# Eight experts on one core: b1 as eight rows with one-pass transposes, and a last piece of w2 of 128 columns

## The chip, the core and the metric

The kernel runs on one core of one Trainium2 chip. The metric is the device time of one execution in microseconds. A core has a matrix engine (TensorE, in the profile PE, with its weight loads as PEld), a vector engine (VectorE, DVE), an activation engine (ScalarE, ACT), GpSimd (POOL), a sync engine (SP), and 16 DMA engines that move data between the device memory and the on-chip memory. TensorE writes only to an accumulator memory (PSUM), from which VectorE or ScalarE copy. Transfers are issued by SP, ScalarE and GpSimd; in the profile an issue stands under SPq, ACTq or POOL.

## The reference

Eight experts, each with 256 rows of tokens, a hidden size of 512 and an inner size of 2,048:

```python
n_experts, capacity, hidden, expert_hidden = 8, 256, 512, 2048

def reference(x, w1, w2, b1, b2):
    h = np.matmul(x, w1) + b1[:, np.newaxis, :]
    h = np.maximum(h, 0)
    return (np.matmul(h, w2) + b2[:, np.newaxis, :]).astype(np.float32)
```

All inputs are float32. w1 and w2 are 4 MB each per expert, 64 MB in all eight.

## The kernel before

The weights are cast to float16 by the transfer that loads them, which GpSimd issues. For each expert x is transposed on TensorE, the first product is made transposed, so that its bias b1 is one number per partition and can go into ScalarE's Relu, and the second product starts from b2. The second product lags three experts behind the first.

b1 has to stand with its 2,048 values of an expert over 128 partitions and 16 columns (`b1T`). It is loaded as 16 rows of 1,024 (each expert's row in two halves) and turned by 32 products with an identity, each of which gives 64 partitions:

```python
b1_rows = singles.tile([E * 2, M // 2], fp32)
b1T = singles.tile([P, nJ, E], fp32)
...
x32 = singles.tile([P, nXF32, nTB, H], fp32)
for e in range(nXF32):      # the first two experts' x, as float32
    (nc.sync if e == 0 else nc.scalar).dma_start(out=x32[:, e], max_dma_last_dim=2048, in_=...)
nc.scalar.dma_start(out=b1_rows, in_=b1.rearrange("e (s i) -> (e s) i", s=2))
load_w1(0)
...
pb = psum_x.tile([P, nJ, E, 2], fp32, tag="psx", name="pb")
for j in range(nJ):                                          # nJ = 16
    for s in range(2):
        ordered(nc.tensor.matmul(                            # L194
            out=pb[s * 64 : (s + 1) * 64, j, :, :],
            lhsT=b1_rows.rearrange("r (q j) -> r q j", j=nJ)[:, :, j],
            rhs=ident[0 : 2 * E, 0 : 2 * E],
            start=True, stop=True,
        ))
for s in range(2):
    nc.vector.tensor_copy(                                   # L202
        out=b1T[s * 64 : (s + 1) * 64, :, :], in_=pb[s * 64 : (s + 1) * 64, :, :, s]
    )
transposes(0)                                                # L97, then the copy to xT in L103
```

The w2 of the last expert comes in six pieces (rows `lo` to `hi` of its 16 per partition, columns `c0` to `c1`), the last two of which share the same rows and split the columns. HH is 256, half of the 512 columns:

```python
for lo, hi, c0, c1 in (
    (0, 4, 0, H), (4, 8, 0, H), (8, 12, 0, H), (12, 14, 0, H),
    (14, 16, 0, HH), (14, 16, HH, H),
):
    t = w2t_pool.tile([P, hi - lo, c1 - c0], fp16, ...)
    ordered(nc.gpsimd.dma_start(out=t, in_=src[:, lo:hi, c0:c1]))       # L90
    w2_sb[e].append((lo, hi, c0, c1, t))
```

The second product of the last expert keeps the same two column blocks in separate accumulators, so every row of the earlier pieces gives two matmuls, one for each block. A block is stored as soon as its last piece is through:

```python
blocks = [(0, HH, psum_o, "po"), (HH, H, psum_h, "ph")]      # e == E - 1
...
for lo, hi, p0, p1, t in w2_sb[e]:
    mine = [b for b in blocks if p0 <= b[0] and b[1] <= p1]
    for tb in range(nTB):                                    # nTB = 2
        for j in range(lo, hi):
            for c0, c1, _, _ in mine:
                ordered(nc.tensor.matmul(                    # L163
                    out=acc[c0, tb],
                    lhsT=hT[e][:, j, tb * P : (tb + 1) * P],
                    rhs=t[:, j - lo, c0 - p0 : c1 - p0], ...))
    if hi == nJ:
        for c0, c1, _, _ in mine:
            store(e, [acc[c0, tb] for tb in range(nTB)], c0, c1, e == E - 1)

def store(e, po, c0, c1, split):
    ...
    nc.vector.tensor_copy(out=out_sb[:, 0, :], in_=po[0])    # L130
    nc.scalar.copy(out=out_sb[:, 1, :], in_=po[1])           # L131
    if split:                                                # the last expert
        nc.sync.dma_start(out=dst[:, 0, :], in_=out_sb[:, 0, :])      # L134
        nc.scalar.dma_start(out=dst[:, 1, :], in_=out_sb[:, 1, :])    # L135
    else:
        nc.sync.dma_start(out=dst, in_=out_sb)               # L137
```

Of the kernel before, what the change touches and what calls it, by code (L numbers as in the profile page):

```python
# [11 lines left out]
def kernel(  # L12
# [9 lines left out]
    nc = tc.nc  # L22
    fp32 = mybir.dt.float32
    fp16 = mybir.dt.float16
    E, T, H = x.shape
    M = w1.shape[2]
    P = 128
    nTB = T // P
    nKC = H // P
    nJ = M // P  # L30
    HH = H // 2
    LAG = 3
    nXF32 = 2

    def ordered(ins):
        return tc.keep_in_program_order(ins)

    singles = ctx.enter_context(tc.tile_pool(name="singles", bufs=1))
# [7 lines left out]
    psum_x = ctx.enter_context(tc.tile_pool(name="psum_x", bufs=1, space=bass.MemoryType.PSUM))  # L46
    psum_h = ctx.enter_context(tc.tile_pool(name="psum_h", bufs=3, space=bass.MemoryType.PSUM))
    psum_o = ctx.enter_context(tc.tile_pool(name="psum_o", bufs=2, space=bass.MemoryType.PSUM))

    ident = singles.tile([P, P], fp32)  # L50
    ident16 = singles.tile([P, P], fp16)
    ones1 = singles.tile([1, P], fp16)
    b2_sb = singles.tile([1, E * H], fp16)
    b1_rows = singles.tile([E * 2, M // 2], fp32)
    b1T = singles.tile([P, nJ, E], fp32)

    x16 = [None] * E
# [11 lines left out]
    def load_w1(e):  # L69
        w1_sb[e] = w1_pool.tile([P, nKC, M], fp16, tag="w1", name="w1sb")  # L70
        ordered(nc.gpsimd.dma_start(  # L71
            out=w1_sb[e], in_=w1[e].rearrange("(p kc) m -> p kc m", kc=nKC)
        ))

    def load_w2(e):
        src = w2[e].rearrange("(p j) h -> p j h", j=nJ)
        w2_sb[e] = []
        if e < E - 1:
            t = w2_pool.tile([P, nJ, H], fp16, tag="w2", name="w2sb")
            step = nJ if e < E - 2 else nJ // 2  # L80
            for lo in range(0, nJ, step):
                ordered(nc.gpsimd.dma_start(out=t[:, lo : lo + step, :], in_=src[:, lo : lo + step, :]))  # L82
                w2_sb[e].append((lo, lo + step, 0, H, t[:, lo : lo + step, :]))
            return
        for lo, hi, c0, c1 in (
            (0, 4, 0, H), (4, 8, 0, H), (8, 12, 0, H), (12, 14, 0, H),
            (14, 16, 0, HH), (14, 16, HH, H),
        ):
            t = w2t_pool.tile([P, hi - lo, c1 - c0], fp16, tag=f"w2_{lo}_{c0}", name=f"w2_{lo}_{c0}")
            ordered(nc.gpsimd.dma_start(out=t, in_=src[:, lo:hi, c0:c1]))  # L90
            w2_sb[e].append((lo, hi, c0, c1, t))

    def transposes(e):
        pt = psum_x.tile([P, nKC, T], fp16, tag="psx", name="psx")
        for kc in range(nKC):
            for tb in range(nTB):
                ordered(nc.tensor.transpose(  # L97
                    out=pt[:, kc, tb * P : (tb + 1) * P],
                    in_=x16[e][:, tb, :].rearrange("p (q kc) -> p q kc", kc=nKC)[:, :, kc],
                    identity=ident16,  # L100
                ))
        xT[e] = xT_pool.tile([P, nKC, T], fp16, tag="xT", name="xT")
        nc.vector.tensor_copy(out=xT[e], in_=pt)  # L103
# [23 lines left out]
    def store(e, po, c0, c1, split):  # L127
        w = c1 - c0
        out_sb = out_pool.tile([P, nTB, w], fp32, tag=f"out{w}", name=f"out{w}")
        nc.vector.tensor_copy(out=out_sb[:, 0, :], in_=po[0])  # L130
        nc.scalar.copy(out=out_sb[:, 1, :], in_=po[1])  # L131
        dst = out[e].rearrange("(p tb) h -> p tb h", tb=nTB)[:, :, c0:c1]
        if split:
# [5 lines that stand above are left out]
    def second_product(e):  # L139
        if e < E - 1:  # L140
            blocks = [(0, H, psum_o, "po")]
        else:
            blocks = [(0, HH, psum_o, "po"), (HH, H, psum_h, "ph")]
        acc = {}
        for c0, c1, pool, tag in blocks:
            for tb in range(nTB):
                t = pool.tile(
                    [P, c1 - c0], fp32, tag=tag if tag == "ph" else f"{tag}{tb}", name=f"acc{tb}"
                )
                acc[c0, tb] = t  # L150
                ordered(nc.tensor.matmul(  # L151
                    out=t,
                    lhsT=ones1,
                    rhs=b2_sb[0:1, e * H + c0 : e * H + c1],
                    start=True,
                    stop=False,
                ))
        for lo, hi, p0, p1, t in w2_sb[e]:
            mine = [b for b in blocks if p0 <= b[0] and b[1] <= p1]
            for tb in range(nTB):  # L160
# [5 lines that stand above are left out]
                            rhs=t[:, j - lo, c0 - p0 : c1 - p0],  # L166
                            start=False,
                            stop=(j == nJ - 1),
# [5 lines that stand above are left out]
    x32 = singles.tile([P, nXF32, nTB, H], fp32)  # L174
    for e in range(nXF32):
        (nc.sync if e == 0 else nc.scalar).dma_start(out=x32[:, e], max_dma_last_dim=2048, in_=x[e].rearrange("(p tb) h -> p tb h", tb=nTB))
    nc.scalar.dma_start(out=b1_rows, in_=b1.rearrange("e (s i) -> (e s) i", s=2))
    load_w1(0)
    ordered(nc.gpsimd.dma_start(  # L179
        out=b2_sb,  # L180
        in_=b2.rearrange("e h -> (e h)").rearrange("(o f) -> o f", o=1),
# [6 lines left out]
        x16[e] = x_pool.tile([P, nTB, H], fp16, tag="x16", name="x16")  # L188
        nc.vector.tensor_copy(out=x16[e], in_=x32[:, e])  # L189

    pb = psum_x.tile([P, nJ, E, 2], fp32, tag="psx", name="pb")
    for j in range(nJ):
        for s in range(2):
            ordered(nc.tensor.matmul(  # L194
                out=pb[s * 64 : (s + 1) * 64, j, :, :],
                lhsT=b1_rows.rearrange("r (q j) -> r q j", j=nJ)[:, :, j],
                rhs=ident[0 : 2 * E, 0 : 2 * E],
                start=True,
                stop=True,
            ))  # L200
    for s in range(2):
        nc.vector.tensor_copy(  # L202
            out=b1T[s * 64 : (s + 1) * 64, :, :], in_=pb[s * 64 : (s + 1) * 64, :, :, s]
        )
    transposes(0)

    loads = []
    for s in range(1, E + LAG):
        if s < E:
            if s >= nXF32:  # L210
                loads.append((load_x, s))
            loads.append((load_w1, s))
        if s >= LAG:
            loads.append((load_w2, s - LAG))
# [8 lines left out]
    for s in range(E + LAG):  # L223
        issue_until(lambda: (
            (min(s + 2, E - 1) < E and w1_sb[min(s + 2, E - 1)] is not None)
            and (s + 2 < LAG or w2_sb[min(s + 2 - LAG, E - 1)] is not None)
        ))
        if s < E:
            first_product(s)
        if s >= LAG:  # L230
            second_product(s - LAG)
# [30 lines left out]
```

## Time and profile before

| | |
|---|---|
| time, median of 3 | 186.09 us (185.63 to 186.1) |
| span of the profiled execution | 183.9 us |
| TensorE busy | 138.5 us (75%) |
| ScalarE busy | 62.8 us (34%) |
| VectorE busy | 13.4 us (7%) |
| read from device memory | 71.39 MB |
| written to device memory | 4.19 MB |

The profile is of one execution, and its span begins and ends somewhat inside the timed interval. Its page has a picture of the span in 40 slices, in which each digit is the busy share of a slice in tenths, and the row DMA is the mean over the 16 DMA engines. GB/s and packet sizes count the bytes as written, so a weight that is read as float32 and written as float16 counts half. The queues: q0 is what GpSimd issues, q1 what SP issues, q10 what ScalarE issues. The timeline gives instructions in order of time: start, duration, engine, line, operation, what it writes and reads, shape, count, and in brackets the idle time of the engine before it with what ended it. The ends of matmuls are modelled: they are pipelined, so that a new one starts long before the one before it has ended in the record.

### The profile page before, as it was taken

How to read it: one execution, taken by the hardware profiler on the slowest of the kernel's cores; microseconds unless marked ns; L12 is line 12 of the kernel's file. 1: busy time of each engine (PE TensorE's matmuls, PEld its weight loads, DVE VectorE, ACT ScalarE, POOL GpSimd, SP SyncE). 2: the span in 40 equal slices, each digit the busy share in tenths (PEclk: the TensorE clock that was granted, in tenths of full speed). 3: DMA queues.
4: the chain of work that ended last, by engine and by line, in shares of the span. 5: the costliest groups of instructions: out<-in, count | busy, mean ns of one | idle time of the engine just before them, and what ended most of it. 6: DMA issues, size and time to landing. Idle time of an engine off the chain costs nothing.

```text
span 183.9 us, 2209 instructions
## 1 busy us (share of the span) xinstructions
PE 138.5 (75%) x946; PEld 99.0 (54%) x946; DVE 13.4 (7%) x22; ACT 62.8 (34%) x138; POOL 16.9 (9%) x37
## 2 busy tenths in 40 slices
PE   0546969397571999529995499917999997999971
PEld 0634969396451846427465464815648842434760
DVE  0320101001000100001010101001010010101001
ACT  0022869477360513605126150622506901010101
POOL 7100030301100012000110000100006200000000
PEclk9999999999875699965999789995799999999998
DMA  5998999899998999899999999999899998999993
GB/s 185 286 221 180 228 228 224 174 229 230 228 217 182 228 228 228 178 278 217 196 214 236 270 203 203 228 271 228 185 228 228 211 275 198 237 243 257 217 211 114
DMA packets 6488, 40.57 MB, mean 221 GB/s; under 512 B 688, under 2 KB 1728, under 8 KB 4432
## 3 DMA queue, kind: packets, MB, share of 16 engines
q0 software_dynamic: 4320, 35.14, 91.3%
q1 hardware_dynamic: 1568, 4.46, 6.6%
q10 hardware_dynamic: 592, 0.85, 1.3%
q8 instruction: 7, 0.11, 0.2%
q14 instruction: 1, 0.01, 0.0%
HBM read 71.39 MB, written 4.19 MB: 411 GB/s over the span
## 4 chain that ended last, share of the span: by engine, by line
DMA 57%; PE 31%; another core or an unknown queue 5%; POOL 3%; issue 1%; ACT 0%; ACTq 0%; POOLq 0%
DMA x<-in_x_dram 25%; DMA w<-in_w_dram 19%; PE ph L110 16%; DMA w1sb<-in_w_dram 12%; PE acc L163 12%; PE psx L97 2%; PE acc L151 1%; POOL w2sb L82 1%; POOL w L90 1%; POOL w1sb L71 1%; ACT out L131 0%; POOL b_sb L179 0%; POOL ident masks.py:199 0%; ACTq L135 0%
## 5 line engine op out<-in xcount | busy, mean ns | idle before, releaser
L110 PE MATMUL ph<-xT,w1sb 128*128 128x256 f16 x512 | 69.3, 302 | 11.8 <-DMA w1sb<-in_w_dram 11.8
L117 ACT ACTIVATE hT<-ph,b1T 128x256 f16<-128x256 f32 x128 | 57.1, 475 | 47.4 <-PE ph L110 47.1
L110 PEld LDWEIGHTS <-w1sb 128*128 128x128 f16 x512 | 62.0, 149 | 18.5 <-DMA w1sb<-in_w_dram 12.8
L163 PE MATMUL acc<-w2sb,hT 128*128 128x512 f16 x224 | 49.7, 379 | 1.5 <-DMA w2sb<-in_w_dram 1.5
L163 PEld LDWEIGHTS <-hT 128*128 128x128 f16 x288 | 27.5, 98 | 32.0 <-issue 6.5
L131 ACT COPY out<-acc 128x512 f32<-128x512 f32 (+1 forms) x9 | 4.9, 541 | 59.7 <-PE acc L163 59.7
L97 PE MATMUL psx<-ident,x 128*128 128x128 f16 x64 | 6.8, 269 | 20.6 <-DMA x<-in_x_dram 20.0
L97 PEld LDWEIGHTS <-x 128*128 128x128 f16 x64 | 5.3, 128 | 21.7 <-DMA x<-in_x_dram 20.9
L103 DVE COPY xT<-psx 128x1024 f16<-128x1024 f16 x8 | 5.5, 692 | 84.3 <-PE psx L97 84.3
L130 DVE COPY out<-acc 128x512 f32<-128x512 f32 (+1 forms) x9 | 5.7, 632 | 74.0 <-PE acc L163 73.9
L71 POOL DMA_DIRECT2D w1sb<-in_w_dram x8 | 4.4, 554 | 67.9 <-PE ph L110 67.1
L82 POOL DMA_DIRECT2D w2sb<-in_w_dram x8 | 4.3, 536 | 57.1 <-PE acc L163 57.1
L194 PE MATMUL pb<-ident,b_rows 16*64 16x16 f32 x64 | 3.7, 266 | 6.4 <-DMA b_rows<-in_b_dram 6.4
L163 PE MATMUL acc<-w,hT 128*128 128x256 f16 x64 | 7.6, 272 | 1.2 <-DMA w<-in_w_dram 1.2
L194 PEld LDWEIGHTS pb<-ident,b_rows 16*64 16x64 f32 x64 | 3.6, 198 | 6.4 <-issue 6.4
L117 ACT ACT_TABLE_LOAD x1 | 1.3, 1283 | 10.9 <-DVE b1T L202 10.9
L151 PE MATMUL acc<-b_sb,ones 1*128 1x512 f16 (+1 forms) x18 | 4.8, 355 | 0.0
L90 POOL DMA_DIRECT2D w<-in_w_dram x6 | 3.6, 614 | 12.4 <-DMA w2sb<-in_w_dram 12.4
L65 POOL DMA_DIRECT2D x<-in_x_dram x6 | 3.3, 546 | 2.2 <-DMA w1sb<-in_w_dram 2.2
L151 PEld LDWEIGHTS <-ones 1*128 1x128 f16 x18 | 1.1, 92 | 2.1 <-issue 2.1
L189 DVE CAST x<-x 128x1024 f16<-128x1024 f32 x2 | 1.4, 698 | 4.3 <-DMA x<-in_x_dram 4.3
L202 DVE COPY b1T<-pb 64x128 f32<-64x128 f32 x2 | 0.6, 288 | 3.5 <-PE pb L194 3.5
(8 smaller groups left out, 2.0 us busy)
## 6 DMA issues: line engine op xcount, KB each, us to landing
w1sb<-in_w_dram POOLq DMA_DIRECT2D x8, 2048.0 KB, 33.6
w2sb<-in_w_dram POOLq DMA_DIRECT2D x6, 2048.0 KB, 47.0
out_dram<-out SPq DMA_DIRECT2D x7, 512.0 KB, 8.0
w2sb<-in_w_dram POOLq DMA_DIRECT2D x2, 1024.0 KB, 24.3
x<-in_x_dram POOLq DMA_DIRECT2D x6, 256.0 KB, 39.9
w<-in_w_dram POOLq DMA_DIRECT2D x3, 512.0 KB, 31.8
x<-in_x_dram ACTq DMA_DIRECT2D x1, 512.0 KB, 5.2
x<-in_x_dram SPq DMA_DIRECT2D x1, 512.0 KB, 4.5
```

Of the source, the lines that this page charges most:

```text
L71: ordered(nc.gpsimd.dma_start(out=w1_sb[e], in_=w1[e].rearrange("(p kc) m -> p kc m", kc=nKC)))
L82: ordered(nc.gpsimd.dma_start(out=t[:, lo : lo + step, :], in_=src[:, lo : lo + step, :]))
L90: ordered(nc.gpsimd.dma_start(out=t, in_=src[:, lo:hi, c0:c1]))
L97: ordered(nc.tensor.transpose(out=pt[:, kc, tb * P : (tb + 1) * P], in_=x16[e][:, tb, :].rearrange("p (q kc) -> p q kc", kc=nKC)[:, :, kc] ...
L103: nc.vector.tensor_copy(out=xT[e], in_=pt)
L110: ordered(nc.tensor.matmul(out=ph, lhsT=w1_sb[e][:, kc, :].rearrange("p (q j) -> p q j", j=nJ)[:, :, j], rhs=xT[e][:, kc, :], start=(kc == 0),
L117: nc.scalar.activation(out=hT[e][:, j, :], in_=ph, func=mybir.ActivationFunctionType.Relu, bias=b1T[:, j, e : e + 1], scale=1.0,)
L130: nc.vector.tensor_copy(out=out_sb[:, 0, :], in_=po[0])
L131: nc.scalar.copy(out=out_sb[:, 1, :], in_=po[1])
L151: ordered(nc.tensor.matmul(out=t, lhsT=ones1, rhs=b2_sb[0:1, e * H + c0 : e * H + c1], start=True, stop=False,))
L163: ordered(nc.tensor.matmul(out=acc[c0, tb], lhsT=hT[e][:, j, tb * P : (tb + 1) * P], rhs=t[:, j - lo, c0 - p0 : c1 - p0], start=False, sto ...
L194: ordered(nc.tensor.matmul(out=pb[s * 64 : (s + 1) * 64, j, :, :], lhsT=b1_rows.rearrange("r (q j) -> r q j", j=nJ)[:, :, j], rhs=ident[0 ...
```

## The change

Two things change. b1 is loaded as eight rows of 2,048, one per expert, and turned by 16 transposes, each of which fills all 128 partitions, so one VectorE copy takes the result. This is meant to shorten the work on TensorE ahead of the first product. And the two last pieces of the last w2 are of 384 and 128 columns in place of 256 and 256, and so are the two column blocks and the stores. This is meant to leave less work behind the piece that lands last.

```diff
-    HH = H // 2
+    HN = H - P
...
-    b1_rows = singles.tile([E * 2, M // 2], fp32)
+    b1_rows = singles.tile([E, M], fp32)
...
-            (14, 16, 0, HH), (14, 16, HH, H),
+            (14, 16, 0, HN), (14, 16, HN, H),
...
-            blocks = [(0, HH, psum_o, "po"), (HH, H, psum_h, "ph")]
+            blocks = [(0, HN, psum_o, "po"), (HN, H, psum_h, "ph")]
...
-    nc.scalar.dma_start(out=b1_rows, in_=b1.rearrange("e (s i) -> (e s) i", s=2))
+    nc.scalar.dma_start(out=b1_rows, in_=b1)
...
-    pb = psum_x.tile([P, nJ, E, 2], fp32, tag="psx", name="pb")
+    pb = psum_x.tile([P, nJ, E], fp32, tag="psx", name="pb")
     for j in range(nJ):
-        for s in range(2):
-            ordered(nc.tensor.matmul(
-                out=pb[s * 64 : (s + 1) * 64, j, :, :],
-                lhsT=b1_rows.rearrange("r (q j) -> r q j", j=nJ)[:, :, j],
-                rhs=ident[0 : 2 * E, 0 : 2 * E],
-                start=True,
-                stop=True,
-            ))
-    for s in range(2):
-        nc.vector.tensor_copy(
-            out=b1T[s * 64 : (s + 1) * 64, :, :], in_=pb[s * 64 : (s + 1) * 64, :, :, s]
-        )
+        ordered(nc.tensor.transpose(
+            out=pb[:, j, :],
+            in_=b1_rows.rearrange("r (q j) -> r q j", j=nJ)[:, :, j],
+            identity=ident[0:E, 0:E],
+        ))
+    nc.vector.tensor_copy(out=b1T, in_=pb)
     transposes(0)
```

## The prediction

> **What bounds the kernel now.** I read the page's second part first, for which resource is full over the whole span.
>
> ```profile
> PE   0546969397571999529995499917999997999971
> DMA  5998999899998999899999999999899998999993
> DMA packets 6488, 40.57 MB, mean 221 GB/s; under 512 B 688, under 2 KB 1728, under 8 KB 4432
> q0 software_dynamic: 4320, 35.14, 91.3%
> q1 hardware_dynamic: 1568, 4.46, 6.6%
> q10 hardware_dynamic: 592, 0.85, 1.3%
> ```
>
> The row DMA is at 8 or 9 tenths in every slice but the first and the last, while TensorE (PE) has slices with 3, 1 and 2 tenths. The three queue lines sum to 99.2% of the time of 16 engines. So the transfers are the bound from about 4 us to about 178 us. The packet records of the trace say the same when packets in flight are counted per microsecond: between 16.0 and 19.9 in every microsecond from 3 to 178. Work off the DMA engines can then only matter at the two ends: before the first weights land, and after the last.
>
> The timeline of the first 16 us shows the first end.
>
> ```profile
> 5.26 1.41 DVE L189 CAST x<-x 128x1024 f16<-128x1024 f32 x2 [4.27 <-DMA x<-in_x_dram]
> 6.44 3.72 PE L194 MATMUL pb<-ident,b_rows 16*64 16x16 f32 x64 [6.44 <-DMA b_rows<-in_b_dram]
> 10.20 0.59 DVE L202 COPY b1T<-pb 64x128 f32<-64x128 f32 x2 [3.53 <-PE pb L194]
> 10.84 1.04 PE L97 MATMUL psx<-ident,x 128*128 128x128 f16 x8 [0.69 <-DVE b1T L202]
> 11.92 0.69 DVE L103 COPY xT<-psx 128x1024 f16<-128x1024 f16 x1 [1.13 <-PE psx L97]
> 15.52 0.61 PEld L110 LDWEIGHTS <-w1sb 128*128 128x128 f16 x4 [3.90 <-DMA w1sb<-in_w_dram]
> ```
>
> Columns: start, duration, engine, line, what, and in brackets the idle time before with its releaser. The turn of b1 (L194), its copy, and the transposes of x are over at 11.92 + 0.69 = 12.61 us. The first product then waits until 15.52 for w1 of the first expert. There are 15.52 - 12.61 = 2.91 us of slack behind this chain.
>
> The timeline of the last 9 us shows the other end.
>
> ```profile
> 175.77 1.91 PE L163 MATMUL acc<-w,hT 128*128 128x256 f16 x16 [0.73 <-DMA w<-in_w_dram]
> 178.12 1.95 PE L163 MATMUL acc<-w,hT 128*128 128x256 f16 x16 [0.44 <-DMA w<-in_w_dram]
> 179.41 0.90 DVE L130 COPY out<-acc 128x256 f32<-128x256 f32 x2 [9.52 <-PE acc L163]
> 179.63 0.37 ACT L131 COPY out<-acc 128x256 f32<-128x256 f32 x1 [8.13 <-PE acc L163]
> 179.86 0.81 SPq L134 DMA_DIRECT2D out_dram<-out  x2
> 180.03 0.37 ACTq L135 DMA_DIRECT2D out_dram<-out  x1
> 180.44 0.37 ACT L131 COPY out<-acc 128x256 f32<-128x256 f32 x1 [0.44 <-PE acc L163]
> 180.84 0.35 ACTq L135 DMA_DIRECT2D out_dram<-out  x1
> ```
>
> From 178.12 TensorE runs 16 matmuls: 8 on the piece of rows 12 to 14, which it had waited for, 4 on the first half-width piece and 4 on the last. The starts are 0.109 us apart. The only larger step is before the 13th, the first on the last piece: 179.317 to 179.470, which is 0.044 us too much. The last packet of the weight stream ends at 179.156, and 0.31 us from there is 179.47. So the last landing and TensorE's own backlog meet within 0.05 us. After that ScalarE works strictly in order: copy, issue, copy, issue. Its second copy could have begun when the last matmul ended, at 179.795 + 0.272 = 180.07, but begins at 180.44, because the first copy and its issue hold the engine until 180.40. The last issue ends at 180.84 + 0.35 = 181.19, the last store's packets run from 181.83 to 182.38, and the span ends at 183.93, 1.55 us later.
>
> **What the Trainium skill says.** "DMA: Bandwidth & Descriptors", section "Why a DMA increments its semaphore by 16 and not by 1", says a copy is spread over the largest number of engines up to 16 that divides the slowest dimension of both sides. The trace agrees as far as it goes: b1 as 16 rows is 16 packets of 4,096 bytes of 159 ns each. By the rule 8 rows go to 8 engines, 8 KB each; no run shows that yet. The same page's "Specifications" give 512 bytes as the least size for full rate. The trace has weight packets of 512 bytes as written (60 ns) and larger, none smaller; the change brings some of 256. "TensorE: Matmul & The Clock Gate", section "Back-to-back issue gap", puts a warm matmul of N columns at N/2.4 + 2.5 ns: 109 ns for 256, just what the tail shows. I use it for 384 columns (162 ns); for 128 it gives 56 ns, and the trace's eight transposes of 128 columns in the chain at 30.37 us take 0.45/8 = 56 ns.
>
> **The change, part by part.**
>
> *b1 on TensorE.* The 64 records of L194 take 3.72 us, 58 ns each: 32 products in two passes. After: 16 one-pass transposes. At 58 ns that is 0.93 us; doubled, for weight loads of 128 columns in place of 64, 1.9 us. One VectorE copy of 128 partitions, about 0.29 us, replaces two (0.59 us together). So xT is ready 2.1 to 3.1 us sooner, at about 9.5 to 10.5 us. All of it lies in front of the wait for w1, which ends at 15.52 either way. Gain on the path: 0.
>
> *b1 on the DMA engines.* If 8 engines carry 8 KB in place of 4, each has one more 159 ns of work ahead of the weight stream, and the other eight have 159 ns less. Every weight load is spread over all 16 and waits for the slowest, and they never run empty until 178 us, so a lag at the start is still there at the end. Whether it counts depends on which engines finish last. In the microsecond after 178 there are 10.2 in flight on average, and 0.9 in the one after 179, so engines differ by up to 1.3 us at the end, and packets do not carry an engine's name. Between 0 and +0.16 us; I take +0.08.
>
> *The stream of w2.* The last 512 packets per 1 KB read become 256 of 1.5 KB and 256 of 512 bytes. The packets written as 512, 2,048, 4,096, 8,192 and 16,384 bytes took 60, 172, 324, 624 and 1,227 ns: 22 ns plus 0.0735 ns per byte. So 768 bytes should cost 79 ns and 256 bytes 41 ns. Per engine: 16 x 79 + 16 x 41 = 1.92 us, against 32 x 60 = 1.92 us. The last landing stays at 179.47, and the piece before it lands 0.3 us later than now, still ahead of the 4 matmuls that need it at 179.0.
>
> *TensorE at the end.* 8 matmuls of the 12 to 14 piece: 4 x (162 + 56) = 872 ns, against 8 x 109. Then 4 x 162 = 650 ns, in place of 436, which puts the first store's blocks later by 0.21 us. The last piece would start at 178.12 + 0.872 + 0.650 = 179.64, now past the landing at 179.47, so the wait of 0.044 us goes. Last start 179.64 + 3 x 0.056 = 179.81, ending 0.053 us sooner after it than a 256-column one: about 180.03, against 180.07.
>
> *ScalarE.* Its copies take 372 ns for 256 columns and 590 ns for 512 (page groups kept apart by shape): 0.85 ns per column, so about 480 for 384 and 264 for 128; the sum is the same. It starts its first copy at 179.63 + 0.21 = 179.84 and does copy, issue, copy, issue in the same total: last issue ends at 181.19 + 0.21 = 181.40. This is the term that counts: **the path runs through ScalarE's first copy, which waits for more columns than before, not through the last landing.**
>
> *The stores.* The last store shrinks from 128 packets of 1 KB (0.54 us from first start to last end) to 128 of 512 bytes. If it has the engines to itself, it takes about 0.35 us and gives back 0.19 of the 0.21. But all four stores run from 180.69 to 182.38 with the engines busy almost throughout: 32 packets of 47 ns per engine are 1.5 of those 1.69 us, and the total of bytes is unchanged. If the engines are the limit, the end moves with the first store, which starts later by 0.11 (VectorE's copy waits for the first tb block) + 0.13 (557 in place of 424 ns) = 0.24 us. So +0.02 to +0.25; I take +0.12.
>
> Sum: 0 + 0.08 + 0 + 0.12 = +0.20 us. **186.09 + 0.2 = 186.3 us.**
>
> **Rivals.**
> 1. *The short tail pays.* If the last landing is what sets the end, everything behind it shrinks: 4 x 53 ns of matmul, 0.05 of latency, 0.11 of copy, 0.19 of store, about 0.55 us, giving 185.5. For it: the 13th matmul does wait 0.044 us for the landing. Against: ScalarE's second copy waits for ScalarE, 0.37 us past its input.
> 2. *Small packets cost more.* If a packet of 256 bytes written costs as much as one of 512 (60 ns), the stream ends 16 x 19 = 0.3 us later; TensorE has 0.17 us in hand there, and ScalarE 0.7, so most is still hidden. At twice 60 ns, 16 x 79 = 1.26 us later, about 0.4 of which would show past ScalarE's chain: 186.7. No packet below 512 bytes in the weight stream speaks for or against.
> 3. *The start counts.* If the first product began with b1 and not with w1, 2 to 3 us would be gained: 183.5. The idle of 3.90 us in front of L110, released by a DMA, is against it.
> 4. *Fewer instructions.* The queue of instruction fetches moves seven packets of 16 KB, about 0.9 us each, on engines that also carry weights. Some 100 records fewer may shift or save one: plus or minus 0.3 us.
>
> **Range and chances.** My sum is +0.2. Rivals 1, 2 and 4 put the edges at about -0.5 and +0.7, and the three times before are themselves spread from 185.63 to 186.1. Hence 185.6 to 187.0. Two per cent is 3.7 us, more than all the work behind the last landing except the fixed 1.55 us: 0.01 faster, 0.98 the same, 0.01 slower.
>
> **What would show each step.** L97's first transposes near 8 us and L110 still released by w1 at 15.5: the b1 part is hidden. Eight b1 packets of about 310 ns in place of 16 of 159: the spread. Weight packets of about 79 and 41 ns: the linear cost. A first ScalarE copy of about 480 ns from 179.84 (shifted with the landing), a second right behind its issue: the ordered chain. I am wrong if ScalarE's second copy begins when its matmul ends, if L110 begins earlier than 15.3, or if the time between landing of the 12 to 14 piece and the last issue shrinks.

## The result, and the profile after

The changed kernel takes 186.46 us (186.25 to 186.55, 6 runs), beside 185.96 us for the kernel before in runs on the same chip: a ratio of 1.0029, 95% interval 1.0016 to 1.0041. A second series of both on another chip gave 186.45 against 186.07 us, ratio 1.0023 (1.0016 to 1.0030, 21 and 41 runs). By the medians it is slower by 0.4 to 0.5 us, where 0.2 was forecast.

The page of the kernel after, its slices and queues:

```profile
PE   0425999299542999639992599937999994999991
DMA  5999999999999999899999999999999999999983
DMA packets 6472, 40.57 MB, mean 220 GB/s; under 512 B 936, under 2 KB 1720, under 8 KB 4408
q0 software_dynamic: 4320, 35.14, 91.1%
q1 hardware_dynamic: 1568, 4.46, 6.7%
q10 hardware_dynamic: 576, 0.85, 1.3%
```

The DMA engines are as full as before, and the queues sum to 99.1% of the span. Packets under 512 bytes went from 688 to 936: the 256 weight packets of 256 bytes, less 8 small ones that b1 no longer needs. The timeline of its first 16 us:

```profile
7.10 1.90 PE L193 MATMUL pb<-ident,b_rows 8*128 8x8 f32 x16 [7.10 <-DMA b_rows<-in_b_dram]
9.03 0.29 DVE L198 COPY b1T<-pb 128x128 f32<-128x128 f32 x1 [2.02 <-PE pb L193]
9.38 1.04 PE L97 MATMUL psx<-ident,x 128*128 128x128 f16 x8 [0.39 <-DVE b1T L198]
10.46 0.69 DVE L103 COPY xT<-psx 128x1024 f16<-128x1024 f16 x1 [1.14 <-PE psx L97]
15.93 0.40 PEld L110 LDWEIGHTS <-w1sb 128*128 128x128 f16 x3 [5.78 <-DMA w1sb<-in_w_dram]
```

The turn of b1 shrinks from 3.72 to 1.90 us, but begins later, at 7.10 in place of 6.44: its eight rows land later. xT is ready at 11.15 in place of 12.61. TensorE then waits for w1, and the first product begins at 15.93, 0.4 us later than before (in the second profiles of both kernels 15.65 and 15.58). The last 6 us of the same timeline:

```profile
179.37 1.03 PE L163 MATMUL acc<-w,hT 128*128 128x384 f16 x8 [0.22 <-DMA w<-in_w_dram]
179.90 0.76 DVE L130 COPY out<-acc 128x384 f32<-128x384 f32 x2 [8.44 <-PE acc L163]
180.22 0.65 ACT L131 COPY out<-acc 128x384 f32<-128x384 f32 x2 [7.16 <-PE acc L163]
180.48 0.81 SPq L134 DMA_DIRECT2D out_dram<-out  x2
180.73 0.87 ACTq L135 DMA_DIRECT2D out_dram<-out  x2
```

Two things differ from the kernel before. TensorE comes to a stop in front of the 384-column piece and starts again at 179.37, released by its transfer; before, that start stood at 178.99, in an unbroken row of matmuls. And ScalarE does both copies and then both issues, where it used to copy, issue, copy, issue. The stretches behind that (columns: stretch, its length, busy time of PE, PEld, DVE, ACT and POOL, clock, DMA share, GB/s):

```profile
180.50:181.00 0.50, 0.00 (x0) 0.00 (x0) 0.15 (x1) 0.37 (x2) 0.00 (x0) 1.00 0.00 0
181.00:181.50 0.50, 0.00 (x0) 0.00 (x0) 0.00 (x0) 0.00 (x0) 0.00 (x0) 1.00 0.33 114
181.50:182.00 0.50, 0.00 (x0) 0.00 (x0) 0.00 (x0) 0.00 (x0) 0.00 (x0) 1.00 1.06 378
182.00:182.50 0.50, 0.00 (x0) 0.00 (x0) 0.00 (x0) 0.00 (x0) 0.00 (x0) 1.00 0.98 338
182.50:183.00 0.50, 0.00 (x0) 0.00 (x0) 0.00 (x0) 0.00 (x0) 0.00 (x0) 1.00 0.78 219
```

The same stretches of the kernel before:

```profile
180.50:181.00 0.50, 0.00 (x0) 0.00 (x0) 0.00 (x0) 0.31 (x1) 0.00 (x0) 1.00 0.58 195
181.00:181.50 0.50, 0.00 (x0) 0.00 (x0) 0.00 (x0) 0.00 (x0) 0.00 (x0) 1.00 1.02 334
181.50:182.00 0.50, 0.00 (x0) 0.00 (x0) 0.00 (x0) 0.00 (x0) 0.00 (x0) 1.00 1.05 346
182.00:182.50 0.50, 0.00 (x0) 0.00 (x0) 0.00 (x0) 0.00 (x0) 0.00 (x0) 0.88 0.52 174
```

In the changed kernel the first store starts at 181.31, in the kernel before at 180.69. From then on the DMA share is about 1 in both until the last store is through. So the stores take the engines whole, and the moment at which the first of them starts sets the end.

### The profile page after: what moved, and what is told of

It reads as the page before. It is cut to its first block, busy times and chain, and to the rows that moved or that the text cites. A ratio compares the mean times of both kernels' runs of the same rounds, so it can differ in the third digit from the quotient of the medians.

```text
span 184.5 us, 2111 instructions
## 1 busy us (share of the span) xinstructions
PE 138.6 (75%) x898; PEld 97.0 (53%) x898; DVE 13.0 (7%) x21; ACT 62.8 (34%) x138; POOL 16.9 (9%) x37
## 4 chain that ended last, share of the span: by engine, by line
DMA 52%; PE 36%; another core or an unknown queue 7%; POOL 2%; issue 1%; ACT 0%; POOLq 0%
DMA x<-in_x_dram 25%; PE ph L110 21%; DMA w<-in_w_dram 18%; PE acc L163 12%; DMA w1sb<-in_w_dram 8%; PE psx L97 2%; POOL w L90 1%; PE acc L151 1%; POOL w2sb L82 1%; ACT out L131 0%; POOL w1sb L71 0%; POOLq L240 0%
## 5 line engine op out<-in xcount | busy, mean ns | idle before, releaser
L110 PE MATMUL ph<-xT,w1sb 128*128 128x256 f16 x512 | 70.5, 306 | 11.4 <-DMA w1sb<-in_w_dram 11.4
L110 PEld LDWEIGHTS <-w1sb 128*128 128x128 f16 x512 | 62.8, 150 | 18.4 <-DMA w1sb<-in_w_dram 12.1
L163 PE MATMUL acc<-w2sb,hT 128*128 128x512 f16 x224 | 51.2, 388 | 2.6 <-DMA w2sb<-in_w_dram 2.6
L163 PEld LDWEIGHTS <-hT 128*128 128x128 f16 x288 | 26.8, 99 | 34.1 <-issue 8.1
L131 ACT COPY out<-acc 128x512 f32<-128x512 f32 (+2 forms) x9 | 4.8, 541 | 61.0 <-PE acc L163 61.0
L130 DVE COPY out<-acc 128x512 f32<-128x512 f32 (+2 forms) x9 | 5.6, 631 | 76.1 <-PE acc L163 76.1
L163 PE MATMUL acc<-w,hT 128*128 128x384 f16 (+1 forms) x64 | 7.3, 273 | 0.2 <-DMA w<-in_w_dram 0.2
L193 PE MATMUL pb<-ident,b_rows 8*128 8x8 f32 x16 | 1.9, 252 | 7.1 <-DMA b_rows<-in_b_dram 7.1
L193 PEld LDWEIGHTS pb<-ident,b_rows 8*128 8x128 f32 x16 | 1.8, 197 | 7.1 <-issue 7.1
L151 PE MATMUL acc<-b_sb,ones 1*128 1x512 f16 (+2 forms) x18 | 4.8, 355 | 0.0
```

The costliest lines, as they stand in the source:

```text
L110: ordered(nc.tensor.matmul(out=ph, lhsT=w1_sb[e][:, kc, :].rearrange("p (q j) -> p q j", j=nJ)[:, :, j], rhs=xT[e][:, kc, :], start=(kc == 0),
L151: ordered(nc.tensor.matmul(out=t, lhsT=ones1, rhs=b2_sb[0:1, e * H + c0 : e * H + c1], start=True, stop=False,))
L163: ordered(nc.tensor.matmul(out=acc[c0, tb], lhsT=hT[e][:, j, tb * P : (tb + 1) * P], rhs=t[:, j - lo, c0 - p0 : c1 - p0], start=False, sto ...
L193: ordered(nc.tensor.transpose(out=pb[:, j, :], in_=b1_rows.rearrange("r (q j) -> r q j", j=nJ)[:, :, j], identity=ident[0:E, 0:E],))
```

## The experiments

A profile is one execution. The position of one event in it can move: in two profiles of the unchanged kernel before, the last weight packet ends at 179.15 and at 179.47 us. Verdicts on time below rest on the intervals of many runs, and from profiles only distances between events are used. Theory A was that b1 in eight rows makes eight DMA engines late and that this lag reaches the end; rival B that the tail is all of it.

### The tail alone

```diff
 # kernel before, b1 untouched
-    HH = H // 2
+    HN = H - P          # and HN in the pieces and blocks
```

> The kernel before with the last two pieces of w2 of 384 and 128 columns and nothing else; b1 stays 16 rows. Theory A (b1 in eight rows makes eight DMA engines late by some 0.4 us, the lag stays to the end, the new tail adds 0.1 to 0.2): the last weight packet ends at about 179.15 us, as before, and the time is 0.1 to 0.2 us above before. Rival B (all of it is the tail: packets of 256 bytes and the wider first block): the last weight packet ends near 179.5, the time is 0.5 us above before.

Measured: 186.41 against 186.09 us, ratio 1.0015 (1.0009 to 1.0022): +0.17 to +0.41 us, which lies between what theory A and rival B expected. TensorE waits for the 384-column piece here too, until 179.42. The last weight packet ends at 179.44, which lies within what the unchanged kernel does. So the tail alone brings most or all of the loss, and theory A has no more than the rest.

### b1 alone

```diff
 # changed kernel with
-    HN = H - P
+    HN = H // 2
```

> The kernel before with b1 as eight rows and the one-pass transposes, the tail as before (256 and 256 columns). Theory A: the first weight packets of eight engines start 0.2 to 0.3 us after the others and take about 1.5 us in place of 1.23; the last weight packet ends near 179.55; time 0.3 to 0.4 us above before. Rival B: no change from before, within 0.1 us.

Measured: 186.12 against 186.09 us, ratio 1.0003 (0.9994 to 1.0013), that is -0.11 to +0.24 us. No loss that can be seen, so theory A fell as the account of the time. The lag itself is in the packet records: the 16 engines complete the second weight load within 0.25 us of each other in the kernel before (but for one, which is 1.2 us late), while in the changed kernel seven do so within 0.08 us, one at 0.40, and eight from 0.55 to 0.76 us behind. The first weight packets of twelve engines take 1.29 to 1.58 us with b1 alone, in place of 1.23. But the eight rows are not needed for such a lag: in the profile of "All of the first block first" below, where b1 still comes in 16 rows, eight first weight packets take 1.43 to 1.46 us, and half of the engines complete the second weight load 0.48 us or more behind the first one. So what makes the lag is not shown.

### b1 spread over the partitions

```diff
 # changed kernel with
-    b1_rows = singles.tile([E, M], fp32)
+    b1_rows = singles.tile([P, M], fp32)
...
-    nc.scalar.dma_start(out=b1_rows, in_=b1)
+    nc.vector.memset(b1_rows, 0.0)
+    nc.scalar.dma_start(out=b1_rows[0:P:P // E, :], in_=b1)
...      # 16 products, lhsT of 128 partitions, rhs=ident[:, 0:P:P // E]
```

> The changed kernel with the eight rows of b1 put on partitions 0, 16, 32 and so on to 112 in place of 0 to 7 (the tile is zeroed first; the turn is 16 products over 128 partitions with every 16th column of the identity). Still eight engines with 8 KB each. If the lag is only the bytes (0.16 us more than before): first weight packets of the late engines still 1.5 us, time as the changed kernel. If the slow first weight packets come from eight engines writing into eight neighbouring partitions: they take about 1.23 us, the last weight packet ends 0.2 to 0.3 us earlier than in the changed kernel, and so does the run.

Measured: 186.42 against 186.09 us, ratio 1.0013 (1.0005 to 1.0022), the same as the tail alone. As a test of where the lag comes from it is not clean: the load waits for the zeroing and its packets come at 7.2 us, among the weights and not in front of them. The engines then complete the second weight load within 0.29 us of each other. But it shows something else, in its timeline from 9 to 19 us:

```profile
9.40 7.07 PE L194 MATMUL pb<-ident,b_rows 128*128 128x8 f32 x32 [9.40 <-DMA b_rows<-in_b_dram]
17.94 0.69 DVE L103 COPY xT<-psx 128x1024 f16<-128x1024 f16 x1 [1.14 <-PE psx L97]
18.68 0.58 PE L110 MATMUL ph<-xT,w1sb 128*128 128x256 f16 x2 [0.78 <-DVE xT L103]
```

Here b1 does hold up the first product, which starts at 18.68 and is released by VectorE: 2.75 us later than in the changed kernel. The time is not longer for it than with the tail alone. The loads were issued ahead and keep the DMA engines full meanwhile.

### b1 twice

```diff
 # changed kernel, b1_rows now the first 8 of 40 partitions of b1_all
     nc.scalar.dma_start(out=b1_rows, in_=b1)
+    nc.scalar.dma_start(out=b1_all[32 : 32 + E, :], in_=b1)
```

> The changed kernel with b1 loaded a second time in eight rows, to partitions 32 to 39, which nobody reads. Theory A: the same eight engines get another 8 KB and are late by another 0.3 to 0.55 us; the last weight packet ends at 179.9 to 180.1, the time is 0.3 to 0.55 us above the changed kernel (186.8 to 187.0). If only the total of bytes counted, 64 KB over 16 engines would add 0.15 us. Rival C (the placing of instruction fetches, which differs between before and after): no steady addition, within 0.1 us of the changed kernel apart from the 0.15.

Measured: 186.92 against 186.09 us, ratio 1.0041 (1.0028 to 1.0054), the last weight packet ends at 180.02. Beside the tail alone on the same chip (1.0015) the two eight-row loads together cost about 0.0026 x 186 = 0.5 us. For the second by itself there is the changed kernel on other chips: by its ratios (1.0023 and 1.0029) 0.2 to 0.3 us, by its medians nearly 0.5. That is more than the 0.15 of its bytes on 16 engines, though with five runs the difference of the ratios is not clear of 0.15. At the end of the weight stream the engines finish 2.7 us apart in this profile, and 0.8 to 1.2 us apart in all others, those of the kernel before included. So a lopsided load can reach the end, as theory A has it, once it is large enough; the 8 KB per engine of the change itself did not, within the interval. That the first load's lag hides in a spread which is there anyway would fit, but is not shown: the records do not name the engines.

### The last rows in quarters

After these runs I read the packet starts as if packets of 256 bytes followed each other after 45 or 67 ns, theory D, and tested it with four times as many.

```diff
 # kernel before; blocks take their columns from whichever piece has them
-            (14, 16, 0, HH), (14, 16, HH, H),
+            (14, 16, 0, P), (14, 16, P, 2 * P), (14, 16, 2 * P, 3 * P), (14, 16, 3 * P, H),
```

> The kernel before (b1 in 16 rows, blocks and stores of 256 and 256 columns), but rows 14 to 16 of the last w2 come in four pieces of 128 columns: 64 packets of 256 bytes written per DMA engine in place of 32 of 512. Theory D (packets of 256 bytes start 56 ns apart on average although each takes 41 ns, those of 512 bytes 41 ns apart although each takes 60, so that spacing and not duration is the cost): 64 x 56 = 3.6 us per engine in place of 32 x 41 = 1.3; the last weight packet ends at about 181.4, the time is 1.9 to 2.2 us above before (188.1). If durations were the cost: 64 x 41 against 32 x 60, 0.7 us more on the engines and 0.3 to 0.6 in the time. If small packets cost nothing extra: within 0.1 us of before.

Measured: 186.38 against 186.14 us, ratio 1.0012 (1.0003 to 1.0021): +0.06 to +0.39 us, not the 2 us of theory D. It fell, and the reading was at fault: 45 and 67 are two and three times 22.3, distances between packets of several engines. At the end of this stream, where six engines are left, each starts a packet every 22 ns (starts at 178.998, 179.020 and 179.042). In the changed kernel the last engine left alone does the same (179.455, 179.477, 179.500). A packet starts 19 ns before the one ahead of it ends, for 256 bytes (41 ns) as for 512 (60). So 64 x 22 = 1.4 us stands against 32 x 41 = 1.3. What the remaining 0.2 us of this kernel is made of I can't say.

### Only the loads of 384 and 128

```diff
 # kernel before, blocks and stores still 256 and 256
-            (14, 16, 0, HH), (14, 16, HH, H),
+            (14, 16, 0, 3 * P), (14, 16, 3 * P, H),
```

> The kernel before with pieces of 384 and 128 columns, but blocks and stores of 256 and 256 as before (b1 in 16 rows): the second block takes its columns from both pieces. Theory D (the loads are the cost of the tail): the last weight packet ends 0.3 to 0.5 us later than before, TensorE waits about 0.4 us for the piece of 384 columns, and the time is 0.25 to 0.4 us above before, as with the tail alone. Rival E (the wider first block, its copies and its store are the cost): stream and time as before, within 0.1 us.

Measured: 186.35 against 186.14 us, ratio 1.0011 (1.0003 to 1.0019): +0.06 to +0.35 us, rival E's "as before" is out, and so is theory D's reason. TensorE waits for the wider piece until 179.37, as in the changed kernel, though the last weight packet ends no later than in the second profile of the kernel before (table below), and in this profile the first store starts 1.75 us behind that restart. In the changed kernel it is 1.94.

### All of the first block first

```diff
 # kernel before, e == E - 1; d is the piece of rows 12 to 14
-        for lo, hi, p0, p1, t in w2_sb[e]:
+            steps = [(w, blocks) for w in w2_sb[e][:3]]
+            steps += [(d, blocks[:1]), (w2_sb[e][4], blocks[:1])]
+            steps += [(d, blocks[1:]), (w2_sb[e][5], blocks[1:])]
+        for (lo, hi, p0, p1, t), want in steps:
```

> The kernel before, but in the last expert the matmuls of rows 12 to 16 go by blocks: all of the first block (4 matmuls on rows 12 to 14, 4 on its last piece), then all of the second, so that the first store can leave 0.44 us sooner while the same work is done. If the order of copy and issue on ScalarE and the four stores behind it set the end, as I think: first store's packets from about 180.25 in place of 180.69, last ones end at about 182.0 in place of 182.37, time 0.2 to 0.35 us below before. If the last landing alone sets the end: as before, within 0.1 us.

Measured: 186.10 against 186.14 us, ratio 1.0000 (0.9991 to 1.0009). No gain, where I had expected 0.2 to 0.35 us. With the four matmuls on rows 12 to 14 done sooner, TensorE stands waiting for the first block's own piece (a step of 0.37 us in its starts, until 179.21), and the first store starts 1.70 us behind that, at 180.91 and not at 180.25. So the order gives little while the piece lands when it does.

### The changed kernel and the kernel before, again

No edit.

> The changed kernel once more, in more runs, beside the kernel before on the same chip. Theory F: the end is set by the first store, from whose first packet all four stores take 1.67 us with the DMA engines full; the first store waits for the piece of 384 columns, whose last packet ends only 0.38 to 0.57 us ahead of the last weight packet. Expected: time 0.3 to 0.5 us above before; TensorE restarts 0.38 us behind the last packet of the 384-column piece, first store 1.9 to 2.0 us behind that restart, end of the last packet 1.67 us behind the first store's start. Rival B (the last landing sets the end): the last store's end follows the last weight packet by the same 3.2 us as before.

> The kernel before once more, for a second profile: how far the end of the last weight packet moves from one execution to the next with nothing changed. Expected: between 179.0 and 179.5 us, and the distance from there to the last store's end within 0.1 us of 3.2 us.

Measured: the changed kernel 1.0023 (1.0016 to 1.0030). From the packet records, in us:

| | last weight packet ends | first matmul on the first block's last piece | first store starts | last store ends | last weight packet to end |
|---|---|---|---|---|---|
| before | 179.15 | 178.99, no wait | 180.69 | 182.37 | 3.22 |
| before, again | 179.47 | 179.16, waits | 180.86 | 182.52 | 3.05 |
| b1 alone | 179.34 | 178.76, waits | 180.46 | 182.43 | 3.10 |
| after | 179.56 | 179.37, waits | 181.31 | 182.98 | 3.42 |
| after, again | 179.36 | 179.14, waits | 181.07 | 182.75 | 3.39 |
| tail alone | 179.44 | 179.42, waits | 181.36 | 183.03 | 3.58 |
| loads only | 179.40 | 179.37, waits | 181.13 | 182.80 | 3.41 |

In the second profile of the kernel before, two matmuls in front of the first block's last piece start 0.26 us apart in place of 0.11, and the weight loads of TensorE stop there as well:

```profile
179.16 0.42 PEld L163 LDWEIGHTS <-hT 128*128 128x128 f16 x4 [0.16 <-issue]
```

Three distances hold. From the first store's start to the end of the last: 1.66 to 1.68 us in all rows but b1 alone (1.97, where the engines run empty in between). From the first matmul on the piece to the first store: 1.70 to 1.71 us in the three profiles with a block and loads of 256, 1.94 with a block of 384. And that matmul comes 0.32 or 0.58 us ahead of the end of the last weight packet where TensorE waits for a piece of 256, but 0.03 to 0.22 where it waits for one of 384 (0.00 in the spread kernel and with b1 twice, which are not in the table). Theory F holds, and rival B, with the same 3.2 us behind the last landing for both, does not. My 0.1 us for the spread of that distance was too tight: the kernel before has 3.05 and 3.22.

### The first 256 columns ahead of the rest

```diff
 # kernel before
-            (8, 12, 0, H), (12, 14, 0, H),
-            (14, 16, 0, HH), (14, 16, HH, H),
+            (8, 12, 0, H), (12, 16, 0, HH),
+            (12, 14, HH, H), (14, 16, HH, H),
```

> The kernel before with the pieces of the last w2 cut otherwise: rows 12 to 16 of the first 256 columns first, then rows 12 to 14 and rows 14 to 16 of the other 256, in place of rows 12 to 14 of all columns and two pieces of rows 14 to 16. The first block is then complete some 1.3 us ahead of the last landing (32 packets of 512 bytes, 41 ns apart). Theory F: the first store starts 0.5 us sooner against the last weight packet than in the kernel before (about 1.0 us behind it in place of 1.5), the end is then set by ScalarE's second copy and issue, about 3.0 us behind the last weight packet in place of 3.2; time 0.1 to 0.25 us below before. Rival B: no change, within 0.1 us.

Measured: 185.91 against 186.07 us, ratio 0.9988 (0.9981 to 0.9995): faster than both kernels, by 0.1 to 0.35 us against before. Its last timeline:

```profile
179.16 0.37 ACT L131 COPY out<-acc 128x256 f32<-128x256 f32 x1 [6.13 <-PE acc L163]
179.18 1.90 SPq L134 DMA_DIRECT2D out_dram<-out  x2
179.57 0.37 ACTq L135 DMA_DIRECT2D out_dram<-out  x1
180.51 0.37 ACT L131 COPY out<-acc 128x256 f32<-128x256 f32 x1 [0.97 <-PE acc L163]
180.91 0.35 ACTq L135 DMA_DIRECT2D out_dram<-out  x1
```

The first store's packets start at 180.01, 0.44 us behind the last weight packet (179.57) in place of 1.39 to 1.54; I had expected about 1.0. ScalarE's second copy no longer stands behind an issue: it waits 0.97 us for TensorE. Its stretches show that the stores no longer fill the engines:

```profile
180.50:181.00 0.50, 0.00 (x0) 0.00 (x0) 0.21 (x1) 0.37 (x1) 0.00 (x0) 1.00 0.72 246
181.00:181.50 0.50, 0.00 (x0) 0.00 (x0) 0.00 (x0) 0.00 (x0) 0.00 (x0) 1.00 0.00 0
181.50:182.00 0.50, 0.00 (x0) 0.00 (x0) 0.00 (x0) 0.00 (x0) 0.00 (x0) 1.00 0.82 277
```

Half a microsecond at 0.00 lies between the two pairs of stores. The last store ends 2.91 us behind the last weight packet, so here the last landing, with TensorE, one copy and one issue behind it, does set the end.

## Why the prediction was right or wrong

*The number.* I forecast 186.3 us, and 186.46 came. That it is so near is partly luck: my +0.20 was 0.08 for b1, which does not show, and 0.12 for the stores, half of what the records show for them, and the later piece of w2 was missing from it.

*The bound, and b1 on TensorE: right.* TensorE's work ahead of the first product does not count; the spread kernel shows it, with its first product 2.75 us later and a time like that of the tail alone (1.0013 beside 1.0015). The 16 transposes take 1.90 us, the upper of my two figures, and the copy 0.29. xT came at 11.15 and not by 10.5, because I left the start at 6.44 although the load of b1 now takes longer. Rival 3 is out.

*b1 on the DMA engines: the packets are there, the size of the lag and its worth were off.* Eight packets of 8 KB, 309 ns each, are there as foretold. I put the lag at 0.16 us; it is 0.55 to 0.76 at the second weight load, but the one profile without the eight rows that has such a group has 0.48 to 0.59 there. I added 0.08 us to the time; b1 alone adds 0.03, with an interval that holds both nothing and 0.24.

*The stream of w2: right, from a wrong column.* Durations of 79 and 41 ns came out as worked out, and the sum per engine is unchanged. But durations overlap by 19 ns, so an engine spends 22, 41 and 60 ns per packet of 256, 512 and 768 bytes. The sum came out right because 60 + 22 equals 2 x 41, which is luck. Rival 2 is out: a packet of 256 bytes costs less than one of 512.

*"The piece before it lands 0.3 us later than now, still ahead of the 4 matmuls that need it at 179.0": this is the step that failed.* The 0.3 us is right: behind the piece the last one takes 16 x 22 = 0.35 us per engine in place of 16 x 41 = 0.66. The slack was not there. In the profile that I read, TensorE had been held until 178.12 by rows 12 to 14, and its backlog hid the landing. In the second profile of the same kernel it waits for the piece of 256 until 179.16, and in the changed kernel for the piece of 384 until 179.14 and 179.37. Measured against the last weight packet, 0.1 to 0.3 us of the later landing goes onto the path.

*ScalarE: the order and the path were wrong.* In the changed kernel it goes copy, copy, issue, issue. And its first copy, through which I saw the path run, was not what set the end: the first store comes from VectorE's copy (179.90) and SP's issue (180.48), and from its start on the engines are full.

*The stores: the branch that I weighed down.* I had two cases, +0.02 if the last store has the engines to itself and +0.25 if the engines are the limit, and took +0.12. They are the limit: 1.67 us from the first store's start in every kernel with blocks of 384. The 0.24 us for the wider first block (second matmul, longer latency, longer copy on VectorE) is what the records give: 1.94 - 1.70. Together: 0.24, and 0.1 to 0.3 for the later piece (0.32 less 0.03 to 0.22), against a measured 0.3 to 0.56 us in the longer series. I had 0.12 and 0. The split between the two is read from the records and not shown in time: no run has the wider block with the old loads, and the tail alone (+0.17 to +0.41 us) and its loads alone (+0.06 to +0.35) overlap.

*Rivals 1 and 4.* The short tail pays nothing, since the first block's piece and not the last one leads the path. Fetches of instructions are seven, as before, so none was saved. Their placing did move: the last one, 0.88 to 0.89 us on one engine, starts at 165.10 before and at 176.94 in the changed kernel. But with b1 alone it starts at 176.50 and no loss is seen, and with the tail alone at 165.80 and the loss is there. So the placing does not account for the loss.

## What to carry to other kernels

Making the last piece of a stream smaller helps only if the last piece leads the path to the end; here its larger neighbour, with its wider copy and store, did, and the neighbour landed closer to the end as well. Where the final stores fill the DMA engines, ask when the first of them can start, and order the loads so that one output block is complete early: a cut by columns first gained 0.1 to 0.35 us, where narrower last columns lost 0.17 to 0.41. A wait that a profile does not show may only be hidden behind another that happened to end later in that execution.

## What the hardware showed beyond expectation

- In all four profiles with b1 in eight rows of 8 KB ahead of the weights, the first weight packets of nine or more engines were slow: 1.34 to 1.58 us for nine of them in the changed kernel, in place of 1.23. With the rows on every 16th partition, and 2 us later, almost all took 1.23. But in one of seven profiles with b1 in 16 rows eight of them took 1.43 to 1.46 us. The cause is open.
- From the end of a piece's last packet to TensorE's first matmul on it: 0.30 to 0.38 us, in the six profiles with a piece of 384 columns and a wait for it.
- ScalarE's second issue takes 0.46 us where it directly follows its first, as in the changed kernel, and 0.35 where a copy stands between them, as in the kernel before. That SP issues at the same time does not explain it: with b1 alone and with the first 256 columns ahead, SP's second issue overlaps with ScalarE's by 0.17 us, and ScalarE's takes 0.35.
- Sixteen one-pass float32 transposes with weights of 8 rows and 128 columns follow each other after 110 ns. The 64 records of the two-pass products with weights of 16 rows and 64 columns follow after 36 and 75 ns in turn, 111 for a product. So a transpose that fills 128 partitions takes as long as a product that filled 64.
